# Transposing the row factors of the first norm behind the first projection

## The chip, the cores and the metric

The kernel runs on one core of a Trainium2 chip. The metric is device time in microseconds (us), as a median over runs: 1290.21 us before, from three runs between 1290.13 and 1290.51. TensorE (PE) multiplies, VectorE (DVE) and ScalarE (ACT) work on tiles, GpSimd (POOL) and SyncE (SP) mostly issue DMAs. Each engine takes its instructions in order.

## The reference

One layer of an encoder on x of 1024 tokens by 1024 channels, all float32, cut to what matters here:

```
h = x * rsqrt(mean(x*x, channels) + 1e-6) * g_pre_mix     # norm 1
u, q, k, v = split(h @ w_in)            # u: 512 channels, q, k, v: 8 heads of 64
y_pool = (windowed means of u, minus u, @ w_pool_mix, * pool_scale) @ w_br_pool
y_sb   = stick_breaking_attention(q, k, v) @ w_br_sb
gates  = sigmoid(h @ w_gate + b_gate)
x = x + rmsnorm((gates[:1024]*y_pool + gates[1024:]*y_sb) @ w_out) * g_post_mix
x = x + rmsnorm(relu(rmsnorm(x)*g_pre_mlp @ w_up)**2 @ w_down) * g_post_mlp
```

The row factor of norm 1, one number per token, is the rsqrt. It is not needed before the products: the kernel multiplies x by the gain alone, and scales what comes out of each projection by the row factor.

## The kernel before, in words

Channels lie on partitions and tokens along a row, in two halves of 512 tokens. Every float32 product is three matmuls of rounded pieces (high x high, high x low, low x high; `mm3`, L112 to L114). A projection of one group of 128 outputs over one half is `dense_steps`: 8 steps of `mm3`, 24 matmuls.

`phase_in` runs the first stage. ACT and DVE split x into `hT_hi` and `hT_lo` and add the squares over the eight channel tiles into `acc`, one for each half. PE computes groups 0, 1 and 2 of u for half 0 together (first run), then the same groups for half 1 one behind the other (second run, 72 matmuls, tiles `du`, `zu`). Beside the second run stand two calls of `stats(h)`: behind step 2 for half 0, and 14 steps later for half 1. `stats` sums `acc` over partitions with a matmul by ones (`ms`, L332), and `rstd` makes the factors from it: two activations on ACT (L153, L154) and three DVE instructions (L155 to L157) that write `rb[h]`, in which each row holds all factors of the half. Then `stats` transposes four 128x128 blocks of `rb[h]` on PE into `rt` (L336) and copies one column of each into `rcol` (L337): the same factors, one token on each partition.

`rb` scales u (`u_out`, L380), q, k (`job_qk`, L464) and the gates. `rcol` is read by `job_v` alone (L496, L497), which has tokens on partitions.

In PSUM, `ms`, `rt`, the first half of each pooling mix (`dm`, L412 to L419) and later attention's `o` share the tag "o", which has one bank. The tag "d" has two: `du` of group 0, of group 3, `dqk`, `dv` and `dg` take them in turn. Behind the second run come the scaled copies of groups 0 to 2, then group 3 (48 matmuls, two halves) with the first pooling mix between its halves, then q and k of the first pair of heads with the other three mixes, each followed by a store to `yscr`; then attention of head 0 (`z`, `F`, `T`, transposes `at`), with `dv` and the gates' projections `dg` filling PE.

The code is written in the order of priority. A planner with a model of the engines' times sets the final order: on each engine it puts next the instruction of highest priority whose operands and buffers it expects to be there. Tiles of one tag wait until an earlier tile's last reader is done.

Of the kernel before, what the change touches and what calls it, by code (L numbers as in the profile page):

```python
# [49 lines left out]
class Block:  # L50
# [197 lines left out]
    def phase_in(self):  # L248
# [81 lines left out]
        def stats(h):  # L330
            ms = self.zps.tile([P, H], F32, name="ms", tag="o", bufs=1)
            nc.tensor.matmul(ms, self.ones, accs[h], start=True, stop=True)  # L332
            self.rstd(ms, pa, ("sq", 3), out=self.rb[h])
            rt = self.zps.tile([P, H], F32, name="rt", tag="o", bufs=1)
            for j in range(4):
                nc.tensor.transpose(rt[:, j * P : j * P + P], self.rb[h][:, j * P : j * P + P], self.eye)  # L336
            nc.vector.tensor_copy(  # L337
                self.rcol[:, 4 * h : 4 * h + 4].rearrange("p (j o) -> p j o", o=1),
                rt.rearrange("p (j o) -> p j o", o=P)[:, :, 0:1],
            )  # L340
# [12 lines left out]
        def stats_side():  # L353
            yield 2
            stats(0)
            yield 14
            stats(1)
# [18 lines left out]
        def u_out(g, ps):  # L376
            if g not in us:
                us[g] = self.op.tile([P, 1024], F32, name=f"u{g}", tag=f"oT{g}")
            for h, d in ps:
                nc.vector.tensor_mul(us[g][:, h * H : h * H + H], d, self.rb[h])  # L380
# [9 lines left out]
        def pool_group(g):  # L390
            u = us[g]
            cur = u
            for i in range(g + 1):
                sh = 1 << i
                nxt = pb.tile([P, 1024], F32, name="win", tag="win", bufs=3)
                nc.vector.tensor_add(nxt[:, sh:], cur[:, sh:], cur[:, : 1024 - sh])
                nc.vector.tensor_copy(nxt[:, :sh], cur[:, :sh])
                cur = nxt
            w = 1 << (g + 1)
            nc.vector.scalar_tensor_tensor(  # L400
                out=cur[:, w:], in0=cur[:, w:], scalar=1.0 / w, in1=u[:, w:], op0=ALU.mult, op1=ALU.subtract
            )
            nc.vector.tensor_mul(cur[:, :w], cur[:, :w], self.rcnt[:, :w])
            nc.vector.tensor_sub(cur[:, :w], cur[:, :w], u[:, :w])
            return cur

        def pool_mix(g, cur):
            sc = self.vt[:, V_PSC + g : V_PSC + g + 1]
            yl = us[g]
            ph = pb.tile([P, 1024], F32R, name="ph")  # L410
            pq = pb.tile([P, 1024], F32R, name="pq")
            nc.scalar.copy(ph, cur)  # L412
            nc.vector.tensor_sub(pq, cur, ph.bitcast(F32))
            for h in range(2):
                c = slice(h * H, h * H + H)
                d = self.zps.tile([P, H], F32, name="dm", tag=("o", "at")[h], bufs=h + 1)
                self.mm3(d, [(wmh[:, g, :], wml[:, g, :], ph[:, c], pq[:, c])])
                nc.scalar.activation(cur[:, c].bitcast(F32R), d, AF.Copy, scale=sc)
                nc.vector.scalar_tensor_tensor(  # L419
                    out=yl[:, c].bitcast(F32R), in0=d, scalar=sc, in1=cur[:, c], op0=ALU.mult, op1=ALU.subtract  # L420
                )
            for t, scr in zip((cur, yl), self.yscr[g]):
                nc.gpsimd.dma_start(scr.bitcast(F32), t)
# [4 lines left out]
        for h in range(2):  # L428
            d = self.dps.tile([P, H], F32, name="du", tag="d")
            self.dense(d, self.weights(("u", 3)), self.hT[h])  # L430
            u_out(3, [(h, d)])
            if h == 0:
                pool_mix(0, pooled[0])
                pooled.append(pool_group(1))
                u_out(2, list(enumerate(dst[2])))
        self.run(self.job_qk("q", 0, 0))
        pool_mix(1, pooled[1])
        pooled.append(pool_group(2))
# [887 lines left out]
```

## Time and profile before

| | |
|---|---|
| median of 3 runs | 1290.21 us |
| profiled execution | 1291.31 us, of which the span is 1289.5 us |
| PE busy | 1268.3 us (98%), 6145 matmuls |
| DVE busy | 924.2 us (72%) |
| ACT busy | 605.5 us (47%) |
| POOL busy | 175.2 us (14%) |
| DMA | 233.72 MB, 181 GB/s |
| chain that ended last | PE 88%, DVE 6%, DMA 2%, issue 2%, ACT 1% |

The span runs from the first to the last instruction on the chip. Engines work side by side, so busy shares add to more than 100%. A matmul's duration overlaps the next one's: back to back, matmuls of 128x512 last 0.39 us each but start 0.23 us apart, so the starts tell the rate. The chain that ended last is followed back from the last instruction to whatever released it. In a row, the mark `<-` in brackets says how long the engine was idle and what ended that.

### The profile page before, as it was taken

Reading aid. Unit: us, or ns where it says so; the run is one execution under the profiler, and the core shown is the slowest. Engines: PE = TensorE matmul, PEld = TensorE weight load, DVE = VectorE, ACT = ScalarE, POOL = GpSimd, SP = SyncE. Lnnn points to the kernel's source line nnn. Section 1 sums busy time; section 2 is a strip of 40 time slices with the busy share of each in tenths; the row PEclk is TensorE's granted clock in tenths of the full one; section 3 lists DMA queues with packets and bytes.
Section 4 is the critical chain, followed back from the end, with each engine's and each line's share of the span. In section 5 each row is a group of like instructions: output and inputs, shape, how many; then the busy total and the mean of one; then the engine's idle time right before and its main releaser. Section 6 shows DMA issues by size and latency. Waiting matters only on the chain.

```text
span 1289.5 us, 16851 instructions
## 1 busy us (share of the span) xinstructions
PE 1268.3 (98%) x6145; PEld 1063.1 (82%) x6145; DVE 924.2 (72%) x1303; ACT 605.5 (47%) x989; POOL 175.2 (14%) x346
## 2 busy tenths in 40 slices
PE   9899999999999999999999999999999999999996
PEld 6688888998888888888877888888888888888885
DVE  8686587688777756661667979777775655776876
ACT  8145455555555543232446646545554433344341
POOL 1011213202322331000101002211220000001000
PEclk9899999999999999999999999999999999999998
DMA  6152646624837978451338577756569546547641
GB/s 223 50 176 81 225 123 164 131 67 113 214 123 177 296 204 234 158 180 49 136 109 285 184 249 254 244 190 210 190 226 342 186 157 225 190 173 246 239 160 66
DMA packets 75746, 233.72 MB, mean 181 GB/s; under 512 B 8624, under 2 KB 11184, under 8 KB 73488
## 3 DMA queue, kind: packets, MB, share of 16 engines
q1 hardware_dynamic: 47936, 143.64, 33.8%
q0 software_dynamic: 27152, 88.49, 23.1%
q8 instruction: 48, 0.79, 0.3%
q10 hardware_dynamic: 576, 0.52, 0.1%
q14 instruction: 34, 0.28, 0.1%
HBM read 178.10 MB, written 83.89 MB: 203 GB/s over the span
## 4 chain that ended last, share of the span: by engine, by line
PE 88%; DVE 6%; DMA 2%; issue 2%; ACT 1%; SPq 0%; POOL 0%; DVEq 0%; POOLq 0%; ACTq 0%
PE d L114 18%; PE d L112 18%; PE d L113 18%; PE dg L110 5%; PE dg L114 5%; PE dg L113 5%; PE o L606 3%; PE at L581 2%; PE dqk L113 2%; PE dqk L114 2%; PE dqk L110 2%; DMA wraw<-w 2%; PE z L552 1%; PE z L549 1%; DVE wlo L83 1%
## 5 line engine op out<-in xcount | busy, mean ns | idle before, releaser
L113 PE MATMUL d<-blo,whi 128*128 128x512 f32 (+1 forms) x456 | 172.7, 379 | 0.0
L114 PE MATMUL d<-bhi,wlo 128*128 128x512 f32 (+1 forms) x456 | 171.9, 378 | 0.0
L112 PE MATMUL d<-bhi,whi 128*128 128x512 f32 (+1 forms) x456 | 168.4, 378 | 0.0
L562 DVE TENSOR_TENSOR_SCAN F<-F,past 128x384 f32<-128x384 f32 (+3 forms) x96 | 93.5, 974 | 25.8 <-ACT F L553 24.9
L82 ACT CAST whi<-wraw 128x512 fp32r<-128x512 f32 (+1 forms) x88 | 67.7, 799 | 88.5 <-PE d L113 33.9
L110 PE MATMUL dg<-hT_hi,whi 128*128 128x512 f32 x256 | 103.3, 404 | 0.3 <-DVE v L497 0.3
L83 DVE TENSOR_TENSOR wlo<-wraw,whi 128x512 fp32r<-128x512 f32 (+1 forms) x88 | 78.2, 907 | 34.1 <-ACT whi L82 34.1
L113 PE MATMUL dg<-hT_lo,whi 128*128 128x512 f32 x256 | 100.6, 393 | 0.0
L114 PE MATMUL dg<-hT_hi,wlo 128*128 128x512 f32 x256 | 100.4, 392 | 0.0
L113 PEld LDWEIGHTS d<-blo,whi 128*128 128x128 f32 x456 | 85.7, 188 | 16.3 <-issue 0.2
L114 PEld LDWEIGHTS d<-bhi,wlo 128*128 128x128 f32 x456 | 85.8, 188 | 16.0 <-issue 0.2
L112 PEld LDWEIGHTS d<-bhi,whi 128*128 128x128 f32 x456 | 85.5, 188 | 15.9
L553 ACT ACTIVATE F<-z 128x384 f32<-128x384 f32 (+3 forms) x96 | 47.3, 493 | 64.1 <-DVE T L566 38.4
L113 PE MATMUL d<-b_lo,whi 128*128 128x512 f32 x196 | 76.7, 391 | 0.0
L112 PE MATMUL d<-b_hi,whi 128*128 128x512 f32 x196 | 75.6, 390 | 0.0
L114 PE MATMUL d<-b_hi,wlo 128*128 128x512 f32 x196 | 75.3, 392 | 0.1
L1093 DVE TENSOR_TENSOR wlo<-slots_hi,whi 128x1024 fp32r<-128x1024 f32 x29 | 35.5, 1224 | 52.6 <-ACT whi L1091 52.5
L1091 ACT CAST whi<-slots_hi 128x1024 fp32r<-128x1024 f32 x29 | 30.5, 1051 | 84.5 <-PE d L113 64.9
L589 DVE TENSOR_TENSOR alo<-at,ahi 128x512 fp32r<-128x512 f32 (+1 forms) x80 | 50.6, 633 | 26.6 <-ACT ahi L588 25.9
L1091 ACT CAST whi<-slots_lo 128x1024 fp32r<-128x1024 f32 x27 | 28.4, 1052 | 72.9 <-PE d L113 59.2
L566 DVE TENSOR_TENSOR T<-T,F 128x127 f32<-128x127 f32 (+4 forms) x96 | 53.1, 556 | 10.2 <-POOL T L556 4.2
L1093 DVE TENSOR_TENSOR wlo<-slots_lo,whi 128x1024 fp32r<-128x1024 f32 x27 | 33.0, 1222 | 36.7 <-ACT whi L1091 36.7
(305 smaller groups left out, 3335.2 us busy)
## 6 DMA issues: line engine op xcount, KB each, us to landing
wraw<-w SPq DMA_DIRECT2D x80, 512.0 KB, 4.3
wscr<-w POOLq DMA_DIRECT2D x24, 1024.0 KB, 9.4
ext_b<-ascr SPq DMA_DIRECT2D x40, 512.0 KB, 4.4
gscr<-gs POOLq DMA_DIRECT2D x32, 256.0 KB, 4.6
gate<-gscr POOLq DMA_DIRECT2D x16, 512.0 KB, 3.7
pscr<-p SPq DMA_DIRECT2D x32, 256.0 KB, 3.7
braw<-w SPq DMA_DIRECT2D x16, 512.0 KB, 5.4
ascr<-c POOLq DMA_DIRECT2D x32, 256.0 KB, 5.2
```

The costliest lines, as they stand in the source:

```text
L82: nc.scalar.copy(hi[:, c], raw[:, c])
L83: self.last_lo = nc.vector.tensor_sub(lo[:, c], raw[:, c], hi[:, c].bitcast(F32)).ins
L110: nc.tensor.matmul(ps, wh, rh, start=first and i == 0, stop=False)
L112: nc.tensor.matmul(ps, wh, rh, start=first and i == 0, stop=False)
L113: nc.tensor.matmul(ps, wh, rl, start=False, stop=False)
L114: nc.tensor.matmul(ps, wl, rh, start=False, stop=last and i == n - 1)
L553: nc.scalar.activation(f[:, c : c + n], z[:, :n], AF.Sigmoid, scale=-1.0)
L562: nc.vector.tensor_tensor_scan(fr, fr, past[:, c : c + n][:, ::-1], 1.0 if top else f[:, c + n : c + n + 1], ALU.mult, ALU.max)
L566: nc.vector.tensor_mul(tl[:, c:e], tl[:, c:e], f[:, c + 1 : e + 1])
L589: nc.vector.tensor_sub(lo[:, c0:], at[:, c0:], hi[:, c0:].bitcast(F32))
L1091: last_split[0] = nc.scalar.copy(hi, src).ins
L1093: last_split[1] = nc.vector.tensor_sub(lo, src, hi.bitcast(F32)).ins
```

## The change

`stats` is cut in two. Its first part, with `ms` and `rstd`, stays where it was. Its second part, the transposes and the copy into `rcol`, becomes `columns(h)`, called for both halves behind the fourth group of u and before q.

```diff
             ms = self.zps.tile([P, H], F32, name="ms", tag="o", bufs=1)
             nc.tensor.matmul(ms, self.ones, accs[h], start=True, stop=True)
             self.rstd(ms, pa, ("sq", 3), out=self.rb[h])
+
+        def columns(h):
+
             rt = self.zps.tile([P, H], F32, name="rt", tag="o", bufs=1)
             for j in range(4):
                 nc.tensor.transpose(rt[:, j * P : j * P + P], self.rb[h][:, j * P : j * P + P], self.eye)
...
                 pool_mix(0, pooled[0])
                 pooled.append(pool_group(1))
                 u_out(2, list(enumerate(dst[2])))
+        for h in range(2):
+            columns(h)
         self.run(self.job_qk("q", 0, 0))
         pool_mix(1, pooled[1])
```

## Rows read from the trace of the kernel before

**Rows 1.** The page: busy time of PE, and its granted clock in 40 slices
```profile
PE 1268.3 (98%) x6145; PEld 1063.1 (82%) x6145; DVE 924.2 (72%) x1303; ACT 605.5 (47%) x989; POOL 175.2 (14%) x346
...
PEclk9899999999999999999999999999999999999998
```
**Rows 2.** Waits of PE: who waited, for what: us in total, times, longest
```profile
PE rt L336 <- DVE rb L157: 4.6, 1, 4.6
...
PE d L112 <- DVE oT L613: 0.9, 1, 0.9
...
PE dv L112 <- DVE v L497: 0.4, 1, 0.4
```
**Rows 3.** Stretches: length, busy PE, PEld, DVE, ACT, POOL (instructions), clock, DMA share, GB/s
```profile
42.90:47.45 4.55, 0.00 (x1) 0.00 (x1) 3.27 (x5) 1.71 (x3) 0.00 (x0) 0.82 0.21 41
...
48.21:52.63 4.42, 4.42 (x13) 3.44 (x12) 4.42 (x10) 0.00 (x0) 0.00 (x0) 0.50 0.02 8
52.63:61.30 8.67, 8.67 (x39) 7.14 (x38) 7.58 (x13) 1.07 (x2) 0.00 (x0) 1.00 0.01 2
```
**Rows 4.** PE in order of time: start us, us, what
```profile
36.38 0.60 PE L336 MATMUL rt<-eye,rb 128*128 128x128 f32 x4
36.73 0.48 PE L114 MATMUL zu<-hT_hi,wlo 128*128 128x512 f32 x1
...
41.40 1.02 PE L332 MATMUL ms<-acc,ones 128*128 128x512 f32 x2
...
42.50 0.40 PE L114 MATMUL zu<-hT_hi,wlo 128*128 128x512 f32 x1
47.45 1.11 PE L336 MATMUL rt<-eye,rb 128*128 128x128 f32 x4 [4.55 <-DVE rb L157]
48.21 0.77 PE L112 MATMUL du<-hT_hi,whi 128*128 128x512 f32 x1
...
52.63 0.40 PE L113 MATMUL du<-hT_lo,whi 128*128 128x512 f32 x1
```
**Rows 5.** DVE in order of time, from the factors of half 0 to L380
```profile
29.77 0.69 DVE L155 SCALAR_TENSOR_TENSOR nb<-ms,rb 128x512 f32<-128x512 f32 x1
30.37 0.68 DVE L328 TENSOR_TENSOR acc<-acc,sq 128x512 f32<-128x512 f32 x1
...
31.69 0.69 DVE L157 SCALAR_TENSOR_TENSOR rb<-nb,rb 128x512 f32<-128x512 f32 x1
...
37.02 0.16 DVE L337 COPY rcol<-rt 128x4 f32<-128x4 f32 x1 [3.50 <-PE rt L336]
...
46.70 0.69 DVE L157 SCALAR_TENSOR_TENSOR rb<-nb,rb 128x512 f32<-128x512 f32 x1
47.31 1.28 DVE L380 TENSOR_TENSOR u<-du,rb 128x512 f32<-128x512 f32 x2
```
**Rows 6.** First pooling mix, in order of time; last row: readers of rcol (min/median/max ns, first start)
```profile
59.07 1.21 DVE L413 TENSOR_TENSOR pq<-win,ph 128x1024 fp32r<-128x1024 f32 x1
...
65.61 0.39 PE L113 MATMUL dm<-pq,wmh 128*128 128x512 f32 x1
...
66.99 1.41 DVE L419 SCALAR_TENSOR_TENSOR u<-dm,vt,win 128x512 fp32r<-128x512 f32 x2 [3.40 <-ACT win L418]
...
L496 ACT ACTIVATE v<-dv,rcol x16: 467/475/502, 90.2 to 304.9; 128x256 fp32r<-128x256 f32 x16
```
**Rows 7.** Start of attention, DVE and PE in order of time
```profile
110.48 0.68 DVE L566 TENSOR_TENSOR T<-T,F 128x512 f32<-128x512 f32 x1
...
114.88 0.38 PE L581 MATMUL at<-eye,T 128*128 128x128 f32 x2
```
**Rows 8.** Stretches of the pooling stage, columns as in rows 3
```profile
47.31:61.30 13.99, 13.85 (x52) 11.35 (x53) 12.90 (x24) 1.07 (x2) 0.00 (x0) 0.81 0.07 29
61.30:77.00 15.70, 15.70 (x71) 13.01 (x70) 11.84 (x16) 7.45 (x12) 1.11 (x2) 1.00 0.29 104
77.00:94.75 17.75, 17.34 (x100) 15.05 (x98) 17.47 (x30) 7.46 (x12) 1.74 (x4) 1.00 0.70 200
```

## The prediction

> **What bounds the kernel now.** Read the engine shares first: TensorE (PE) is busy 98% of the span, and its granted clock is full except in the second and the last of 40 slices [rows 1]. So only time in which PE waits or runs slowly is worth anything. The list of who waited for whom on PE comes next, and it is short: one wait of 4.6 us, on the transposes `rt` for `rb`; in the whole kernel behind it none is over 0.9 us, and in the stage that follows the longest is 0.4 us, `dv` for `v` [rows 2]. The reader is to see that one line of code holds the only large wait in the kernel.
>
> The stretches around it show the clock too. In the 4.55 us of the wait the mean granted clock falls to 0.82, so it fell inside the wait; from 48.21 to 52.63 us it is 0.50, which is 1.2 GHz; behind that it is 1.00, 2.4 GHz [rows 3]. What PE did before it fell is the wait. The cost is therefore the wait and the slow matmuls behind it.
>
> Last, PE's own order of time [rows 4]: the first set of four transposes (half 0) stands at 36.38 us among matmuls, the sum over channels of half 1 (`ms`) at 41.40, the last matmul of the third projection group at 42.50, then nothing until the transposes of half 1 at 47.45, and only then the fourth group `du`. The matmuls of `du` do not need the transposes: they need weights and an output bank. They stand behind them on an in-order queue.
>
> **The change part by part.** It takes eight transposes with their eight weight loads and two copies of 128x4 out of `stats` and issues the same ones behind the fourth group. No instruction is added or dropped, and no DMA moves; SP's and POOL's queues are not touched. On PE the transposes pass the rest of the second run, the 48 matmuls of `du` and, in program order, the six of the first pooling mix; on DVE the copies pass the eight scaled copies L380, two pooling groups and the first mix.
>
> *The restart of PE.* Behind the last `zu` matmul (42.50) the next could start 0.23 us later, at 42.73. The transposes started at 47.45: 4.72 us lost. They took 0.76 us (47.45 to 48.21) where the same four took 0.35 us at full clock (36.38 to 36.73): 0.41 us. Ten matmuls from 48.21 to 52.63 took 4.42 us; the 38 behind them took 8.67 us, 0.228 each [rows 3, 4], so ten cost 2.28 at full clock: 2.14 us lost. Sum 4.72 + 0.41 + 2.14 = 7.27 us. The transposes still run somewhere, at 0.35 us a set, which this sum has already counted.
>
> *What is late next: the bank for `du`.* Both banks of `du` hold group 0 until DVE's scaled copy (L380) empties them, and in the trace that copy stands behind the whole chain of half 1: `rb` ends at 46.70 + 0.69 = 47.39, the copies start at 47.31 [rows 5]. If that chain stayed there, taking the transposes away would gain almost nothing. I say that it moves, because of the bank named "o", of which there is one. `ms` of half 0, `rt` of half 0 and `ms` of half 1 take it in turn. The chain of half 0 stands: `rb` ends 31.69 + 0.69 = 32.38, its transposes come at 36.38, 4.0 us later; the copy out of them ends 37.02 + 0.16 = 37.18, and `ms` of half 1 comes at 41.40, 4.2 us later [rows 4, 5]. The planner that fixes the order thus places PE work some 4 us behind the operand that it needs; a third case is the pooling mix, whose operand ends at 60.28 and which comes at 65.61, 5.3 us later [rows 6]. Without `rt` in between, the bank is free when L155 of half 0 has read it, 29.77 + 0.69 = 30.46, and the sum of squares of half 1 is complete at 30.37 + 0.68 = 31.05 [rows 5]. With 4.2 to 5.3 us behind that, `ms` comes at 35.3 to 36.4. Its place in the program allows that: 30 of the 72 matmuls of that run are left behind it, and 42.73 less 30 x 0.228, less 0.87 for `ms` itself (42.50 - 41.40, less one matmul) and 0.35 for `rt`, is 34.7. From `ms` to the end of `rb` took 47.39 - 41.40 = 5.99 us (a weight split on ACT and DVE lies inside). So `rb` of half 1 ends at 41.3 to 42.4, the first scaled copy at 42.0 to 43.1, and PE, with `rt` of half 0 gone, is free at 42.38. The remaining gap is 0 to 0.7 us; I take 0.3. PE gaps of 0.4 us show no fall of the clock behind them [rows 2, 8], so this one costs only itself.
>
> *The end of the pooling stage.* From 77.00 to 94.75 us DVE is the full engine, 17.47 of 17.75 us, and PE's one wait there, 0.4 us, is for DVE to empty a bank of `dv` [rows 2]. PE now comes 7.27 us earlier to that point; DVE's work starts with `rb` of half 1, 4.9 to 6.1 us earlier than 47.39. The difference, 1.2 to 2.4 us, is given back at `dv` unless DVE has slack on the way. It has: 1.09 us idle from 47.31 to 61.30 and 3.86 from 61.30 to 77.00 [rows 8], most of the latter one wait of 3.4 us in the first mix [rows 6]. So the cost is 0 to 2.4 us; I take 0.6, nearer the end at which the slack takes it up.
>
> *The moved copies.* `rcol` is first read at 90.2 us [rows 6], with all of the q and k projections between; a copy of 0.16 us some 20 us earlier costs nothing by itself, and if that cover went, PE would stall only after it had filled both banks of `dv`.
>
> *Sum.* 7.27 - 0.3 - 0.6 = 6.4 us. The profiled execution took 1291.31 us, of which 1.8 lie outside its span, and is 1.1 us above the median of 1290.21; so 1284.9 on its scale and 1290.21 - 6.4 = 1283.8 us as a median. Best of this case: no gap, no loss, and the 0.4 us at `dv` gone too, 7.7 us, 1282.5. Worst: 7.27 - 0.7 - 2.4 = 4.2 us, 1286.0.
>
> **Rivals.** *The order stays.* Something other than the bank holds `ms` of half 1 at 41.40, or the scaled copies stay behind the old place of `rb`. Then `du` starts when the first copy ends, about 48.0 instead of 48.21, still at 1.2 GHz; with a set of transposes at full clock the gain is 0.2 + 0.4 = 0.6 at most, 1289.6 to 1290.2. For it: the copies do stand right behind `rb` in the trace, although half 0's factors were there at 32.38. Against it: three cases in which PE follows a freed operand by 4 to 5 us. A form between: `rb` comes 2 us late and the clock falls all the same; 7.27 - 2 - 2.14 = 3.1, 1287.1.
>
> *The bank "o" is now short in the pooling stage (slower).* The first mix, both `rt` sets and the second mix now share that one bank. A set of transposes held it from 36.38 until `ms` followed at 41.40, 5.0 us [rows 4]; two of them set between the mixes put the later mixes 10.0 us behind, while PE is 7.27 ahead. The mixes feed the stores whose memory the first attention scores take over, so attention starts 2.7 us later than before. It decides from the point at which the delay is more than PE has other work for. The first transposes of attention follow their operand (110.48 + 0.68 = 111.16) at 114.88, 3.7 us [rows 7]; if that is all the cover, 10.0 - 3.7 = 6.3 us of the gain go and it comes out at 1289.2; if the later stages don't hide even that, all 10.0 are lost and the time is 1290.21 - 7.27 + 10.0 = 1292.9. For it: the three mixes behind are a chain through that bank. Against it: slots go to what is ready, and the mix is ready only at 60.28, so both sets may be through before it; and PE has the whole `dv` and `dg` work to do while attention waits. The Trainium skill (Perfetto Trace Analysis, section Matmuls) speaks for this rival: independent matmul groups should rotate through different PSUM banks, so that one can be emptied while the next runs; here they are led through one. No row before shows a mix waiting on a transpose; by that rule alone the time would be this rival's, by the rows on `dv` and DVE it would be the forecast's.
>
> **How the numbers follow.** A measurement of this kernel tells changes over about 0.2%, 2.6 us, from none. Forecast 0.72; the form between 0.05; the order stays 0.08; the bank short, partly covered 0.06, uncovered 0.09. Faster: 0.72 + 0.05 = 0.77; same: 0.08 + 0.06 = 0.14; slower 0.09. The range reaches from the best of the forecast, 1282.4, over the form between to just short of the covered rival, 1289.0: the rest holds under 2 in 10. The forecast's own range is 1282.5 to 1286.0.
>
> **What would show it.** Right: no PE wait above 1 us between 24 and 60 us; `ms` of half 1 near 36 us; granted clock 1.00 from 43 to 53; `du` starting at 42.4 to 43.1; matmuls behind that some 7 us earlier, still so at the end. Wrong: `ms` still at 41, or `du` waiting for L380 (the order stays); later mixes less than 7 us earlier, the first finished `T` of attention (110.48 before, [rows 7]) at or behind its old time, and new PE waits between 90 and 200 us (the bank); a wait on `dv` of over 2.4 us (DVE).

## The result, and the profile after

The change takes the median from 1290.21 us (five runs, 1289.94 to 1290.53) to 1283.57 us (five runs, 1282.74 to 1284.39): 6.6 us less, ratio 0.9945 with a 95% interval of 0.9932 to 0.9959, which is 5.3 to 8.8 us. Run again in another session, the same kernel had a median of 1283.09 us beside 1290.79 us of before, ratio 0.9941 (0.9928 to 0.9953). Forecast were 1283.8 us.

The page of the profiled execution after, busy time and granted clock; they answer to [rows 1].

```profile
span 1281.0 us, 16852 instructions
...
PE 1264.7 (99%) x6145; PEld 1061.3 (83%) x6145; DVE 924.0 (72%) x1303; ACT 605.9 (47%) x989; POOL 175.3 (14%) x346
...
PEclk9999999999999999999999999999999999999998
```

Each engine has as many instructions as before. PE's busy time fell by 3.6 us; 0.41 + 2.14 = 2.55 us of that are the transposes and the ten matmuls that took longer behind the old wait. The second slice of the clock is full now. The list of PE's waits, which answers to [rows 2], has lost its first entry, and the waits of 0.4 and 0.3 us on `v` in the stage behind are gone too:

```profile
PE idle L307 <- DVE zero L304: 1.4, 1, 1.4
PE d L112 <- DVE oT L618: 0.9, 1, 0.9
PE ms L1205 <- DVE acc L1242: 0.8, 1, 0.8
PE du L114 <- DVE wlo L290: 0.7, 1, 0.7
PE du L112 <- ACT whi L289: 0.4, 1, 0.4
PE du L113 <- DVE hT_lo L320: 0.2, 1, 0.2
```

PE in order of time, after, where [rows 4] shows the old order: `ms` of half 1, the restart with `du`, the end of group 4, the transposes.

```profile
34.74 1.02 PE L332 MATMUL ms<-acc,ones 128*128 128x512 f32 x2
...
41.77 0.39 PE L114 MATMUL zu<-hT_hi,wlo 128*128 128x512 f32 x1
41.99 0.39 PE L112 MATMUL du<-hT_hi,whi 128*128 128x512 f32 x1
...
52.65 0.39 PE L114 MATMUL du<-hT_hi,wlo 128*128 128x512 f32 x1
...
67.16 0.60 PE L339 MATMUL rt<-eye,rb 128*128 128x128 f32 x4
67.51 0.48 PE L112 MATMUL dm<-ph,wmh 128*128 128x512 f32 x1
...
74.22 0.60 PE L339 MATMUL rt<-eye,rb 128*128 128x128 f32 x4
78.60 0.40 PE L112 MATMUL dm<-ph,wmh 128*128 128x512 f32 x1
```

`ms` of half 1 stands 6.66 us earlier than in [rows 4], 6.4 us earlier when counted from the first `ms` of either run (34.74 - 25.21 = 9.53 us behind it, where it was 41.40 - 25.50 = 15.90), and `du` follows the last `zu` after 0.22 us, the pace of back-to-back matmuls. DVE, which answers to [rows 5]: the factors of half 1 are done at 40.17 + 0.69 = 40.86, and the scaled copies that free the banks of `du` follow at once; the first ends at about 41.5, half a microsecond before PE wants the bank. The copies into `rcol` come where DVE has time, at 69.77 and 74.89, with their first reader at 81.47.

```profile
40.17 0.69 DVE L157 SCALAR_TENSOR_TENSOR rb<-nb,rb 128x512 f32<-128x512 f32 x1
40.78 1.28 DVE L383 TENSOR_TENSOR u<-du,rb 128x512 f32<-128x512 f32 x2
...
69.77 0.15 DVE L340 COPY rcol<-rt 128x4 f32<-128x4 f32 x1
...
74.89 0.16 DVE L340 COPY rcol<-rt 128x4 f32<-128x4 f32 x1
```

Two stretches after (columns as in rows 3): PE is without a gap at full clock in both, and DVE, full from 77 to 95 us before [rows 8], now has slack there. As PE is some 8 us ahead, the stretch that answers to the old one is rather 69 to 87 us: DVE is busy there for 15.10 of 18 us, where it was 17.72, and PE has no gap.

```profile
42.50:53.00 10.50, 10.50 (x48) 8.71 (x47) 10.50 (x18) 1.73 (x3) 0.00 (x0) 1.00 0.14 51
...
77.00:95.00 18.00, 18.00 (x136) 17.31 (x135) 14.35 (x23) 7.91 (x13) 2.13 (x4) 1.00 0.39 147
```

The stage before the first `ms` differs from one profiled execution to the next, whatever the kernel: the first `ms` (half 0) starts between 25.0 and 26.9 us. So traces are compared here from that instruction on. From it to the end of the span it was 1289.5 - 25.5 = 1264.0 us before, and 1281.0 - 25.2 = 1255.8, 1282.8 - 26.9 = 1255.9 us in the two profiled executions of the changed kernel: 8.2 us less. The medians of the runs say 6.6 and 7.7 us; the interval of either (5.3 to 8.8 and 6.1 to 9.3 us) holds all three figures.

### The profile page after: what moved, and what is told of

Same layout as the page of the kernel before. It is cut to its first block, busy times and chain, and to the rows that moved or that the text cites. A ratio compares the mean times of both kernels' runs of the same rounds, so it can differ in the third digit from the quotient of the medians.

```text
span 1281.0 us, 16852 instructions
## 1 busy us (share of the span) xinstructions
PE 1264.7 (99%) x6145; PEld 1061.3 (83%) x6145; DVE 924.0 (72%) x1303; ACT 605.9 (47%) x989; POOL 175.3 (14%) x346
## 4 chain that ended last, share of the span: by engine, by line
PE 97%; DVE 1%; DMA 1%; ACT 0%; issue 0%; SPq 0%; DVEq 0%
PE d L114 20%; PE d L112 20%; PE d L113 20%; PE dg L114 5%; PE dg L110 5%; PE dg L113 5%; PE o L611 3%; PE at L586 2%; PE dqk L114 2%; PE dqk L113 2%; PE dqk L110 2%; PE z L557 1%; PE z L554 1%; PE dv L114 1%; PE dv L113 1%; PE dv L110 1%
```

## The experiments

**Which transposes matter.** The first two kernels move one half each. The edit is shown against the changed kernel.

```diff
 def stats(h):
     ...
     self.rstd(ms, pa, ("sq", 3), out=self.rb[h])
+    if h == 1:          # second kernel: if h == 0
+        columns(1)      # second kernel: columns(0)
 ...
-for h in range(2):
-    columns(h)
+columns(0)              # second kernel: columns(1)
```

> Only the transposes of half 0 go behind the fourth group; those of half 1 stay in stats. Theory (the bank "o" held by rt of half 0 is what makes ms of half 1, and with it rb of half 1, late): ms of half 1 moves from 41.4 to about 35 us, rb is done near 41, the transposes of half 1 in front of du find it done, no PE wait over 0.5 us there, clock 1.00 behind; 1283 to 1285 us. Rival (what costs is that transposes of half 1 stand in front of du on PE's in-order queue): the wait of 4.6 us stays, 1289 to 1291 us.

Measured: 1283.19 us, ratio 0.9945 (0.9933 to 0.9958), the whole gain. `ms` of half 1 starts at 34.60 us. PE in order of time, moving half 0 only: the transposes of half 1 stand directly in front of `du`, as before the change, and cost their 0.35 us.

```profile
41.63 0.39 PE L114 MATMUL zu<-hT_hi,wlo 128*128 128x512 f32 x1
41.86 0.60 PE L341 MATMUL rt<-eye,rb 128*128 128x128 f32 x4
42.21 0.48 PE L112 MATMUL du<-hT_hi,whi 128*128 128x512 f32 x1
```

> Only the transposes of half 1 go behind the fourth group; those of half 0 stay in stats. Theory (the bank): ms of half 1 stays near 41.4, rb near 47.4, and du now waits for DVE's scaled copy instead, PE waits 4 to 5 us again and the clock falls; 0.2 + 0.4 = 0.6 us at most are gained, 1289.5 to 1290.5 us. Rival (the transposes in front of du are the cost): no wait, 1283 to 1285 us.

Measured: 1292.71 us, ratio 1.0018 (1.0009 to 1.0027): no gain, and 2.2 us worse than before. PE in order of time, moving half 1 only: the transposes are gone from in front of `du`, and `du` waits just as long for DVE's scaled copy, which is line 385 here.

```profile
41.96 1.02 PE L332 MATMUL ms<-acc,ones 128*128 128x512 f32 x2
...
43.05 0.40 PE L114 MATMUL zu<-hT_hi,wlo 128*128 128x512 f32 x1
48.70 0.76 PE L112 MATMUL du<-hT_hi,whi 128*128 128x512 f32 x1 [5.25 <-DVE u L385]
```

The two settle it. The transposes that PE waited at are not the ones whose move pays. It is the transposes of half 0, which show no wait in the list, that make everything of half 1 late; that they do it through the bank is what the next kernel tests. That the second is slower than before, where a gain of up to 0.6 us was foreseen, goes with 13 slow matmuls instead of ten and with PE waits of 1.0 us on `dv` and 0.5 us on `z` behind.

**The bank alone.** The kernel before, with `rt` in other banks and nothing else changed:

```diff
-rt = self.zps.tile([P, H], F32, name="rt", tag="o", bufs=1)
+rt = self.zps.tile([P, H], F32, name="rt", tag="at", bufs=2)
```

> The transposes stay in stats, but rt gets the tag at (two banks, one of which is free then) in place of o. That lets ms of half 1 go at about 35 us, and the order that was built puts the transposes of half 1 right behind it, ahead of the last 24 zu matmuls. Theory (a freed bank is worth only what PE's order makes of it): PE comes to those transposes near 36.5 us, rb of half 1 is done near 41, so the wait moves forward, 4 to 5 us, with the clock falling behind it; no gain, 1289 to 1291 us. Rival (the bank alone is the whole cause, wherever the transposes stand): 1283 to 1285 us.

Measured: 1289.27 us, ratio 0.999 (0.9981 to 0.9999). PE in order of time with the other bank: the bank is free and `ms` is early, 9.5 us behind the first `ms` as after the change, though the transposes of half 0 are still on PE. But the transposes of half 1 stand in the middle of the second run, and PE waits there for factors that are done 3.78 us later, at the price of the clock again.

```profile
35.09 1.02 PE L332 MATMUL ms<-acc,ones 128*128 128x512 f32 x2
...
36.89 0.60 PE L336 MATMUL rt<-eye,rb 128*128 128x128 f32 x4
41.27 1.12 PE L336 MATMUL rt<-eye,rb 128*128 128x128 f32 x4 [3.78 <-DVE rb L157]
42.03 0.78 PE L112 MATMUL zu<-hT_hi,whi 128*128 128x512 f32 x1
```

So it was the bank that held `ms`, and a free bank is needed and not enough: what waits for the factors must not stand in front of work that doesn't.

**The wait and the clock by themselves.** The kernel before, with PE kept busy during the wait:

```diff
     self.finish_side()
+    warm = self.zps.tile([P, H], F32, name="warm", tag="at", bufs=2)
+    for _ in range(18):
+        nc.tensor.matmul(warm, zero[:, :P], zero, start=True, stop=True)
     pa.release()
```

> The kernel before, with 18 matmuls of zeros (bf16, 128x512) between the last zu matmul and the transposes of half 1, where PE waits; nothing else is changed. It splits the loss. Theory: the wait itself (4.7 us) stays, since rb is not earlier, but PE is busy in it, the clock stays at 1.00 and the transposes and the ten matmuls behind them run at full rate: 0.41 + 2.14 = 2.55 us less than before, 1287.2 to 1288.2 us. Rival (the clock falls for another reason, or such matmuls don't hold it): no gain, 1290 to 1291 us.

Measured: 1290.34 us, ratio 1.0002 (0.9994 to 1.0011). No gain, so by the time alone the rival would hold. The trace says otherwise about the clock. PE in order of time:

```profile
43.69 0.40 PE L114 MATMUL zu<-hT_hi,wlo 128*128 128x512 f32 x1
44.15 3.83 PE L368 MATMUL warm<-zero 128*128 128x512 bf16 x17
48.64 0.66 PE L336 MATMUL rt<-eye,rb 128*128 128x128 f32 x4 [0.65 <-DVE rb L157]
49.33 0.47 PE L112 MATMUL du<-hT_hi,whi 128*128 128x512 f32 x1
...
51.70 0.39 PE L113 MATMUL du<-hT_lo,whi 128*128 128x512 f32 x1
```

The first ten matmuls of `du` take 51.70 - 49.33 = 2.37 us where they took 4.42: the clock held, and 2.1 us were won there, with the 0.07 us at the transposes (0.69 us where they took 0.76). Behind it most of the gain disappears: from the first `ms` to the end it is 1290.4 - 26.7 = 1263.7 us, against 1264.0. The list of PE's waits of this kernel shows where:

```profile
PE dv L112 <- DVE qs L467: 1.3, 1, 1.3
...
PE d L112 <- DVE u L1003: 0.5, 1, 0.5
...
PE z L552 <- DVE k L471: 0.2, 1, 0.2
```

The waits on `dv` (at 89.60 us; it was 0.4 before) and on `z` (at 93.86) lie in the stage in which DVE was full: PE arrives there earlier and waits for DVE. Counted from the first `ms`, the last matmul of `dv` starts at 271.51 us, against 272.32 before, so 0.8 of the 2.2 us are left there and 1.4 are gone. The wait of `d` on `u` is another matter: it stands at 769.32 us, in a much later stage, where it and the end of the kernel take most of the rest. That DVE takes the 1.4 us is a new theory, so it was tried: less work for DVE between 60 and 95 us, once without and once with the matmuls of zeros.

```diff
-for i in range(g + 1):
+for i in range(g + 1 if g < 2 else 1):
```

> The kernel before with less work on DVE between 60 and 95 us: pooling groups 2 and 3 make one window sum where they make three and four, so five additions of 1.21 us and five copies of 0.16 are left out, 6.9 us of DVE (the pooled values of these groups are then not the reference's). PE's work is the same. It is the measure for the kernel beside it: 1289 to 1290.5 us, with no wait on dv.

> The same omission, and the 18 matmuls of zeros in the wait of the transposes, which hold the clock at 1.00. With all of DVE's work they won 2.2 us up to the end of du and nothing at the end, with waits on DVE at dv. Theory (DVE, full from 77 to 95 us, took that gain back): with slack on DVE the gain stays, 1.8 to 2.6 us less than its neighbour without the matmuls of zeros. Rival (the gain is lost elsewhere, or was a slow start of that one profiled run): as its neighbour within 0.8 us.

Measured: 1290.88 us without (ratio to before 1.0001, 0.9993 to 1.001) and 1289.54 us with (0.9991, 0.9982 to 1.0): 1.3 us. That is less than the 1.8 expected, and the trace has the reason. PE in order of time, without the matmuls of zeros: the clock comes back after seven starts this time, 48.89 to 51.91, 3.02 us where seven take 7 x 0.228 = 1.60.

```profile
48.89 0.77 PE L112 MATMUL du<-hT_hi,whi 128*128 128x512 f32 x1
...
51.59 0.48 PE L112 MATMUL du<-hT_hi,whi 128*128 128x512 f32 x1
51.91 0.39 PE L113 MATMUL du<-hT_lo,whi 128*128 128x512 f32 x1
```

So 1.4 us were to be had, and 1.3 arrived at the end. With slack on DVE (12.87 of 18 us busy from 77 to 95 in the kernel without the matmuls of zeros, against 17.72 in that stretch before) the clock's part stays; without it, most of it is given back. The traces agree: the last matmul of `dv` starts 270.13 us behind the first `ms` with the matmuls of zeros and 271.55 without, 1.4 us apart, and against the kernel with all of DVE's work and the same matmuls (271.51) it is 1.4 us earlier too. The two intervals overlap, so the size is no better known than that. One thing forecast did not come: both kernels still have a wait of 0.9 us on `dv`, near 107 us, behind the stretch that was relieved; as both have it, it is not in their difference. A side result: leaving out 6.9 us of DVE work alone moved nothing in the median, and PE's wait of 4.55 us in front of it stayed.

**How far the transposes can go.** Two kernels push the change further. One does the columns three times in their place, the other calls them behind all four mixes.

```diff
-for h in range(2):
+for h in (0, 1) * 3:                  # three times
     columns(h)
...
     pool_mix(3, pooled[3])
+    for h in range(2): columns(h)     # last, in place of the call above
     self.run(self.job_qk("k", 0, 1))
```

> The changed kernel once more, as the measure for the two kernels run beside it. Every theory: 1282.7 to 1284.4 us.

> The changed kernel with the two sets of transposes and copies done three times in the same place: four more holds of the bank "o" between the pooling mixes. Theory (attention's late start is covered by dv and dg on PE, as after the change, where F starts 5.2 us earlier than before while PE is some 8 us earlier and no wait follows): only the 16 transposes at 0.35 us a set of four cost, 1.4 us, 1284.6 to 1285.8 us. Rival (the bank short, without cover): four holds of up to 5 us, F starts 10 to 20 us later, PE waits appear between 90 and 200 us; 1290 us or more.

> The changed kernel with the transposes behind all four pooling mixes, so that no mix waits on them. Theory: F of attention starts 1 to 2 us earlier than in the changed kernel (101.6), PE has no wait there either way, the time is the same, 1282.8 to 1284.4 us. Rival (the holds between the mixes cost the changed kernel the 1 to 3 us by which F lags PE's shift): 1281 to 1282.5 us. If rcol comes too late for dv: a PE wait on dv near 85 us and up to 3 us more than the changed kernel.

The changed kernel itself: 1283.09 us. Three times: 1287.36 us, ratio 0.9976 (0.9966 to 0.9986), 4.3 us more. 16 further transposes cost 1.4 of them, by an estimate from 0.35 us for four. `F` of attention starts at 111.37, 9.7 us later than after the change, and the list of PE's waits has three small new ones:

```profile
PE o L611 <- DVE alo L594: 1.0, 1, 1.0
...
PE rt L339 <- DVE rcol L340: 0.3, 1, 0.3
PE dm L112 <- DVE rcol L340: 0.3, 1, 0.3
```

With one of 0.5 us on `d`, far behind at 765 us, these make 2.1 us; 0.8 us of the 4.3 stay open. So neither price was right: four more holds of the bank, with nearly ten further microseconds of delay in attention's start, cost some 3 us beyond the transposes themselves, not nothing and not ten. Two of the waits are for the bank itself, so not all of it comes from attention's start.

Behind all mixes: 1295.4 us, ratio 1.0035 (1.0022 to 1.0049), slower than before the change. `F` is earlier, 100.46, as foreseen, and it does not matter. PE in order of time:

```profile
91.54 0.73 PE L112 MATMUL dm<-ph,wmh 128*128 128x512 f32 x2 [2.97 <-ACT ph L415]
...
95.59 1.11 PE L339 MATMUL rt<-eye,rb 128*128 128x128 f32 x4 [0.71 <-DVE u L422]
96.96 1.11 PE L339 MATMUL rt<-eye,rb 128*128 128x128 f32 x4 [0.26 <-DVE rcol L340]
99.36 0.58 PE L112 MATMUL dv<-whi,hT_hi 128*128 128x256 f32 x1 [1.28 <-DVE v L502]
```

`dv` cannot be emptied before `rcol` is there. From 88.6 to 99.36 us the trace shows no work on PE but the last mix and the transposes, and `dv` goes on only when DVE has emptied a bank of it. From 77 to 127 us PE was idle for 50.00 - 42.15 = 7.85 us at a mean granted clock of 0.90; in the same stretch of the changed kernel it has no gap, at 1.00. The case that `rcol` comes late was foreseen at up to 3 us; it cost 12.3.

## Why the prediction was right

*The restart of PE* was right in its sum. The wait, the slow transposes and the ten slow matmuls are gone, and the sum of 7.27 us with the waits of 0.4 and 0.3 us on `v`, which went too, makes 8.0 of the 8.2 us between the traces. One part has another cause than the text suggests: with the clock held at 1.00 the transposes behind the wait still took 0.69 us, so only 0.07 of their 0.41 us is the clock's. The rest goes with standing behind a wait; where they met none (half 0 moved only) they took 0.35.

*What is late next* was right in its cause, shown by moving either half alone and by giving `rt` another bank: the bank, not the transposes in front of `du`. `ms` of half 1 was put at 35.3 to 36.4, and its place in the program at 34.7. (The code calls `stats` for half 1 behind step 14 of the 24 steps, not 14 steps behind the first call; that is what leaves 30 matmuls.) It came at 34.74, or 25.50 + 9.53 = 35.03 on the time scale of the trace before, with 28 matmuls left behind it. That is near its place, and also 4.0 and 5.3 us behind the end of its last operand in the two traces of the changed kernel, so the runs don't tell whether the planner's distance of some 4 us or the place in the program set it. The gap, taken as 0.3 us, was 0.

*The end of the pooling stage* was taken as 0.6 us lost; nothing was lost, and `dv` did not wait. The mechanism is real all the same: it is what ate most of the gain when only the clock was mended. Here DVE's start moved with PE's, 40.78 - 25.2 = 15.6 us behind the first `ms` in place of 21.8, 6.2 us earlier, and DVE had slack on the way; no run separates the two. The two deductions were too careful by 0.9 us; against the median, 6.6 us, they made the number look closer than the parts were, which is luck.

*The chances.* The prediction says that under 2 in 10 lie outside its range. By its own figures it is 0.08 + 0.06 + 0.09 = 0.23, since 1289.2, 1289.6 to 1290.2 and 1292.9 us all lie above 1289.0.

*The moved copies* cost nothing in the place chosen. The remark that PE would stall once both banks of `dv` are full was right in kind, and the last experiment gives its size.

*The rival on the order* did not come; moving half 1 alone showed what it would have looked like, 1292.71 us where 1289.6 to 1290.2 were given. *The rival on the bank "o"* did happen in part: the second mix is torn in two, one half at 67.51 and the other, behind the second transposes, at 78.60, and `F` of attention starts 106.83 - 101.64 = 5.2 us earlier while PE is over 8 us ahead. The third mix starts at 84.40 us, where it started at 84.88, and the fourth at 95.39 after 98.69, so one of the three signs given for this rival, later mixes less than 7 us earlier, did appear. It cost nothing that the trace shows, since PE had `dv` and `dg` to do: no wait stands between 60 and 330 us. The rule of the Trainium skill (Perfetto Trace Analysis, section Matmuls) that independent groups should rotate through different PSUM banks named the right spot, though for another stage: one bank was the cause of the old wait. But giving `rt` another bank by itself, the remedy closest to the rule, gained 1.2 us (1290.5 to 1289.27, with an interval of 0.1 to 2.5 us); here the order on PE decided the rest.

## What to carry to other kernels

When an engine waits, ask what made the late operand late, back through the buffers: the instruction to move may be one that waits for nobody and holds a bank. A result that is needed late should be taken out of the way of what is needed early, but only as far as its reader's buffers allow: some 27 us later (47.45 to 74.22) was free here, past the last mix cost 12 us. And a gain on the bounding engine stays only if the engine that it meets next comes forward with it or has slack.

## What was not expected

How long the clock stays at 1.2 GHz behind nearly the same wait varied: seven starts in one profiled execution, ten and 13 in others, for waits of 4.55, 4.55 and 5.25 us. The wait of 3.78 us (other bank) brought it down as well, for 12 starts, so the length of the wait does not order them. So did the one of 2.97 us with the short waits behind it (columns last: 0.57 from 91.54 to 99.36 us). And matmuls of zeros held it: with 17 of them recorded in the gap and an idle rest of 0.65 us, the granted clock was 1.00 throughout.
